# Batched matrix product in pairs: product tiles with rows of two batches, and stores of pairs in 16 KB runs

## The chip, the cores and the metric

The kernel runs on one core of a Trainium2 chip. The metric is the device time of one execution in microseconds (us); lower is better. Three runs of the kernel before the change took 125.2 to 125.29 us, with a median of 125.25 us.

Names used below: PE is the matrix engine (TensorE), DVE the vector engine, ACT the scalar engine, POOL GpSimd, and SP the engine that here only issues transfers. SBUF is the on-chip memory with 128 partitions, PSUM the memory that PE writes. DMA engines, sixteen for the core, move data between HBM and SBUF. A transfer is issued from an engine's queue: q10 in the profile is ACT's queue, q1 is SP's.

## The reference

Sixteen independent products of a 512 x 512 matrix with the transpose of another, in float32:

```python
batch, m, k, n = 16, 512, 512, 512
a = randn(batch, m, k)      # float32
b = randn(batch, n, k)      # float32
out = np.matmul(a, b.transpose(0, 2, 1)).astype(np.float32)
```

The inputs are 33.55 MB and the output 16.78 MB.

## The kernel before

The batches go in eight pairs. For a pair, `load` (line 82) brings both batches of `a` in one transfer of 2 MB and both of `b` in another. In both, SBUF partition 64e + p gets the eight consecutive rows 8p to 8p + 7 of batch e of the pair, which is one run of 16 KB; so partitions 0 to 63 belong to the first batch of the pair and 64 to 127 to the second. There are seven slots for loads (`NL`), even numbers being of `a` and odd ones of `b`. Load 1 is issued from SP, all others from ACT: seven at the start, and loads 2u + 7 and 2u + 8 by ACT in pair u, after the copies of line 157 (line 168).

DVE casts what has landed to bfloat16 (lines 130 to 134; `ha` and `wa` are the two halves of the k range of `a`, `hb` and `wb` those of `b`). PE transposes it in blocks of 128 x 128 into PSUM (`tp`, line 199), four groups of 16 transposes for a pair. ACT copies the transposed `a` to `ta` (line 157), DVE the transposed `b` to `tb` (line 144). After a transpose, the 128 columns of a block hold 64 rows of the first batch and 64 rows of the second. The copy of line 157 sorts them: it makes two copies for each block of k, one for each batch, so that in `ta` the rows of one batch stand together.

The product of a batch is made of four tiles of 128 x 512 in PSUM (`ps`, four banks), each a sum over four blocks of k, with `ta` as the stationary operand and `tb` as the moving one (line 218). A pair thus takes 32 matmuls of 128 output rows by 512 columns, the first batch of the pair (e = 0) and then the second. ACT copies each finished tile to the output buffer `ob` (line 177), sorting columns on the way. `ob` is a ring of seven batches (`NO`): before ACT writes batch n, it waits until the store of batch n - 7 has landed (line 174).

A store (line 92) is 1 MB, one for each batch, issued from SP: partition p holds four consecutive rows of the output, a run of 8 KB. SP waits for the counter `s_out`, which ACT raises twice in a pair: after the fifth tile (the first batch is then complete) and after the eighth. Before its first store SP also waits until load 7 has landed (`nc.sync.wait_ge(s_ld[0], 32)`, line 106). The store of the last batch is issued from SP after all compute (line 236).

What sets the order: each engine works through its own instructions in program order, and counters (semaphores) join them. PE's copy-back counters are `s_pv` (tiles of the first batch copied, banks of `ps` free again), `s_ea` and `s_eb` (a block of `ta` or `tb` ready), and its own are `s_mm` (a tile is complete) and `s_ta`, `s_tb` (a group is transposed). SP's queue holds nothing but load 1 and the stores, in order. ACT's holds loads, copies of `ta` and copies of `ob`.

Of the kernel before, what the change touches and what calls it, by code (L numbers as in the profile page):

```python
# [10 lines left out]
def kernel(  # L11
# [6 lines left out]
    nc = tc.nc  # L18
    P = 128
    batch, M, K = a.shape  # L20
    _, N, _ = b.shape
    J = M // P
    KO = K // P
    HP = P // 2
    HK = K // 2
    pairs = batch // 2
    f32 = mybir.dt.float32
    bf16 = mybir.dt.bfloat16
    NL = 7
    NO = 7  # L30

    def sbuf(name, shape, dtype):
        return ctx.enter_context(nc.sbuf_tensor(name, shape, dtype))

    def sem(name):
        return tc.alloc_semaphore(name)

    with tc.tile_critical(no_gpsimd_drain=True):  # L40
        ident = sbuf("ident", [P, P], bf16)
        one = sbuf("one", [P, 1], f32)
        ld = sbuf("ld", [P, NL, 2 * J, K], f32)
        ha, wa, hb, wb = (
            sbuf(name, [P, 2 * J, HK], bf16) for name in ("ha", "wa", "hb", "wb")
        )
        ta = sbuf("ta", [P, KO, 2 * J * P], bf16)
        tb = sbuf("tb", [P, KO, 2 * J * P], bf16)
        ob = sbuf("ob", [P, NO, J, N], f32)
        tp = ctx.enter_context(nc.psum_tensor("tp", [P, 4, 2 * J, P], bf16))  # L50
        ps = ctx.enter_context(nc.psum_tensor("ps", [P, 4, N], f32))

        s_set = sem("s_set")
        s_ld = [sem(f"s_ld{i}") for i in range(NL)]
        s_st = [sem(f"s_st{i}") for i in range(NO)]

        s_go = sem("s_go")
        s_wa = sem("s_wa")
# [6 lines left out]
        s_ea = sem("s_ea")  # L65
        s_eb = sem("s_eb")
        s_mm = sem("s_mm")
        s_pv = sem("s_pv")
        s_out = sem("s_out")
# [5 lines left out]
            out=ident[:], in_=ident[:], compare_op=mybir.AluOpType.not_equal, fill=1.0,  # L75
# [6 lines left out]
        def load(n, engine):  # L82
            u, slot = n // 2, n % NL
            src = (a if n % 2 == 0 else b)[2 * u:2 * u + 2].rearrange(
                "e (p j) k -> (e p) j k", j=2 * J
            )
            engine.dma_start(ld[:, slot], src).then_inc(s_ld[slot], 16)

        def landed(n):
            return s_st[n % NO], 16 * (n // NO + 1)  # L90

        def store(n):
            nc.sync.wait_ge(s_out, n + 1)
            nc.sync.dma_start(
                out[n].rearrange("(p j) n -> p j n", j=J), ob[:, n % NO]
            ).then_inc(landed(n)[0], 16)

        load(0, nc.scalar)
        load(1, nc.sync)
        for n in range(2, NL):  # L100
            load(n, nc.scalar)

        for n in range(2 * pairs):
            nc.gpsimd.wait_ge(s_ld[n % NL], 16 * (n // NL + 1)).then_inc(s_go, 1)  # L104

        nc.sync.wait_ge(s_ld[0], 32)
        for n in range(batch - 1):
            store(n)

        def taker(engine):  # L110
            return lambda s, n: engine.wait_ge(s, n).then_inc(s, -n)  # L111
# [5 lines left out]
        take = taker(nc.vector)  # L117
# [3 lines left out]
        with nc.Fori(0, pairs, engines=[dve]) as u:  # L121
            for x, (h, w, s_c, s_w) in enumerate(
                ((ha, wa, s_ca, s_wa), (hb, wb, s_cb, s_wb))
            ):
                src = ld[:, bass.ds((u * 2 + x) % NL, 1)].rearrange("p o j k -> p (o j) k")
                take(s_go, 1)
                if x == 0:
# [4 lines left out]
                    out=h[:, J:, :], in_=src[:, J:, :HK]  # L132
                ).then_inc(s_c, 1)
                nc.vector.tensor_copy(out=w[:], in_=src[:, :, HK:]).then_inc(s_w, 1)  # L134
            for ko in range(KO):
# [5 lines left out]
                if ko == 1:  # L141
# [3 lines left out]
                    out=tb[:, ko, :],  # L145
                    in_=tp[:, 2 + ko % 2].rearrange("k j p -> k (j p)"),
# [6 lines left out]
        for u in range(pairs):  # L153
            for ko in range(KO):
                nc.scalar.wait_ge(s_ta, KO * u + ko + 1)
                for e in range(2):
                    c = nc.scalar.copy(  # L157
                        out=ta[:, ko, e * J * P:(e + 1) * J * P].rearrange(
                            "k (j p h) -> k j p h", j=J, h=2
                        ),  # L160
                        in_=tp[:, ko % 2, :, e * HP:(e + 1) * HP].rearrange(
                            "k (h j) p -> k j p h", h=2
                        ),
                    )
                c.then_inc(s_ea, 1)


            for n in (2 * u + NL, 2 * u + NL + 1):
                if n < 2 * pairs:
                    load(n, nc.scalar)  # L170
            for e in range(2):
                n = 2 * u + e
                if n >= NO:
                    nc.scalar.wait_ge(*landed(n - NO))
                for j in range(J):
                    nc.scalar.wait_ge(s_mm, J * n + j + 1)
                    c = nc.scalar.copy(  # L177
                        out=ob[:, n % NO, j, :].rearrange("m (p j) -> m p j", j=2 * J),
                        in_=ps[:, j, :].rearrange("m (j p) -> m p j", j=2 * J),
                    )  # L180
                    if e == 0:
                        c.then_inc(s_pv, 1)
                    elif j in (0, J - 1):
                        c.then_inc(s_out, 1)


        pe = nc.tensor.engine
        take = taker(nc.tensor)
        with nc.Fori(0, pairs, engines=[pe]):
            with nc.Fori(0, 2, engines=[pe]):  # L190

                for x, (h, s_c, s_t, s_e) in enumerate(
                    ((ha, s_ca, s_ta, s_ea), (hb, s_cb, s_tb, s_eb))
                ):
                    take(s_c, 1)
                    for g in range(2):
                        take(s_e, 1)
                        for j in range(2 * J):
                            t = nc.tensor.transpose(  # L199
                                tp[:, 2 * x + g, j, :], h[:, j, g * P:(g + 1) * P], ident[:]  # L200
                            )
                            if x == 1 and g == 0 and j == 0:
                                t.then_inc(s_da, 1)
                        t.then_inc(s_t, 1)

            for e in range(2):
                for jj in range(0, J, 2):
                    if e == 1:  # L210
                        take(s_pv, 2)
                    for kk in range(0, KO, 2):
                        for j in (jj, jj + 1):
                            for ko in (kk, kk + 1):
                                if (e, jj, j) == (0, 0, 0) and ko >= 2:
                                    nc.tensor.wait_ge(s_ea, ko - 1)
                                    nc.tensor.wait_ge(s_eb, ko - 1)
                                t = nc.tensor.matmul(  # L218
                                    ps[:, j, :],
                                    ta[:, ko, (e * J + j) * P:(e * J + j + 1) * P],  # L220
                                    tb[:, ko, :].rearrange("k (j p) -> k j p", j=2 * J)[
                                        :, :, e * HP:(e + 1) * HP
                                    ],
                                    start=(ko == 0),
                                    stop=(ko == KO - 1),
                                )
                            if kk == KO - 2:
                                t.then_inc(s_mm, 1)

    with tc.tile_critical(sync_engine=act, no_gpsimd_drain=True):
        for n in range(batch - NO, batch - 1):
            nc.scalar.wait_ge(*landed(n))
    waits = nc.cur_bb.bb.instructions[-1]
    last = nc.sync.dma_start(
        out[batch - 1].rearrange("(p j) n -> p j n", j=J), ob[:, (batch - 1) % NO]
    )
    tc.add_manual_dep(
        last.ins,  # L240
        waits.name,
# [33 lines left out]
```

## Time and profile before

| what | value |
|---|---|
| median of three runs | 125.25 us |
| the profiled execution, its own time | 124.88 us |
| its span, first to last instruction | 123.1 us |
| PE matmuls `ps`, line 218 | 256, mean 379 ns, busy 57.8 us |
| ACT copies `ob`, line 177 | 64, mean 590 ns, busy 34.3 us |
| ACT copies `ta`, line 157 | 64, mean 613 ns, busy 33.0 us |
| PE transposes, line 199 | 512, mean about 224 ns |
| weight loads of the matmuls, line 218 | 256, mean 98 ns |
| read from HBM, written | 33.55 MB, 16.78 MB |
| ACT waiting for a store in the ring of `ob` | 3.8 us, two times |

How to read it: the span runs from the first to the last instruction; the execution's own time is 1.78 us longer. Matmuls are pipelined, so the mean of one is longer than the distance from one to the next: 32 of them end 7.29 us after the first began. Slices of the page are fortieths of the span, about 3.1 us each; a digit is a busy share in tenths. In a line of the timeline stand start, duration, engine, line, operation, output, input, count, and in brackets the idle time before and what ended it. The time of a transfer "to landing" runs from its issue to its completion.

### The profile page before, as it was taken

Reading aid. Unit: us, or ns where it says so; the run is one execution under the profiler, and the core shown is the slowest. Engines: PE = TensorE matmul, PEld = TensorE weight load, DVE = VectorE, ACT = ScalarE, POOL = GpSimd, SP = SyncE. Lnnn points to the kernel's source line nnn. Section 1 sums busy time; section 2 is a strip of 40 time slices with the busy share of each in tenths; the row PEclk is TensorE's granted clock in tenths of the full one; section 3 lists DMA queues with packets and bytes.
Section 4 is the critical chain, followed back from the end, with each engine's and each line's share of the span. In section 5 each row is a group of like instructions: output and inputs, shape, how many; then the busy total and the mean of one; then the engine's idle time right before and its main releaser. Section 6 shows DMA issues by size and latency. Waiting matters only on the chain. (4 is left out here: it accounts for less than half of the span.)

```text
span 123.1 us, 2235 instructions
## 1 busy us (share of the span) xinstructions
PE 90.1 (73%) x768; PEld 54.7 (44%) x768; DVE 67.9 (55%) x96; ACT 67.9 (55%) x130; POOL 0.7 (1%) x6
## 2 busy tenths in 40 slices
PE   0000089999999899989998999999699936997000
PEld 0000078447734764575477447644564425542000
DVE  0000598992896589388918983871987039600000
ACT  0400064567945966696589468855865184666000
POOL 2000000000000000000000000000000000000000
PEclk9999999999999999999999999999999999999965
DMA  4999999999999998999999999999999999999991
GB/s 144 394 426 431 447 437 431 426 431 426 426 431 426 426 405 373 453 399 437 407 429 426 463 405 442 437 415 434 423 418 458 399 426 423 431 429 423 426 431 45
DMA packets 4610, 50.34 MB, mean 409 GB/s; under 512 B 513, under 2 KB 513, under 8 KB 513
## 3 DMA queue, kind: packets, MB, share of 16 engines
q10 hardware_dynamic: 2160, 31.46, 60.6%
q1 hardware_dynamic: 2448, 18.88, 36.4%
q14 instruction: 2, 0.01, 0.0%
HBM read 33.55 MB, written 16.78 MB: 409 GB/s over the span
## 5 line engine op out<-in xcount | busy, mean ns | idle before, releaser
L218 PE MATMUL ps<-tb,ta 128*128 128x512 bf16 x256 | 57.8, 379 | 0.5
L177 ACT COPY ob<-ps 128x512 f32<-128x512 f32 x64 | 34.3, 590 | 26.3 <-PE ps L218 22.5
L157 ACT COPY ta<-tp 128x512 bf16<-128x512 bf16 x64 | 33.0, 613 | 15.5 <-PE tp L199 15.0
L218 PEld LDWEIGHTS ps<-tb,ta 128*128 128x128 bf16 x256 | 24.1, 98 | 30.6 <-issue 4.0
L199 PE MATMUL tp<-ident,ha 128*128 128x128 bf16 x256 | 18.5, 224 | 18.8 <-PEq L111 18.3
L199 PEld LDWEIGHTS tp<-ident,ha 128*128 128x128 bf16 x256 | 15.8, 100 | 22.3 <-issue 20.6
L144 DVE COPY tb<-tp 128x1024 bf16<-128x1024 bf16 x32 | 21.2, 685 | 3.6 <-DVEq L111 3.6
L199 PE MATMUL tp<-ident,hb 128*128 128x128 bf16 x256 | 17.5, 223 | 3.8 <-PEq L111 3.5
L199 PEld LDWEIGHTS tp<-ident,hb 128*128 128x128 bf16 x256 | 15.3, 100 | 5.0 <-issue 4.8
L130 DVE CAST ha<-ld 128x1024 bf16 x8 | 5.5, 690 | 14.6 <-POOLq L104 13.8
L139 DVE COPY ha<-wa 128x2048 bf16<-128x2048 bf16 x8 | 5.5, 691 | 12.4 <-DVEq L111 12.4
L130 DVE CAST hb<-ld 128x1024 bf16 x8 | 5.5, 689 | 8.4 <-DVEq L111 8.4
L134 DVE CAST wa<-ld 128x2048 bf16 x8 | 9.8, 1220 | 0.0
L134 DVE CAST wb<-ld 128x2048 bf16 x8 | 9.8, 1220 | 0.0
L131 DVE CAST hb<-ld 128x1024 bf16 x8 | 5.5, 687 | 0.0
L131 DVE CAST ha<-ld 128x1024 bf16 x8 | 5.5, 687 | 0.0
L143 DVE COPY hb<-wb 128x2048 bf16<-128x2048 bf16 x8 | 5.5, 684 | 0.0
L152 ACT ACT_TABLE_LOAD x1 | 1.3, 1283 | 4.1 <-issue 4.1
L74 POOL TENSOR_SCALAR_AFFINE_SELECT ident<-ident 128x128 bf16<-128x128 bf16 x1 | 0.3, 292 | 0.2 <-POOL ident L72 0.2
L72 POOL MEMSET ident<- 128x128 bf16 x1 | 0.2, 204 | 0.5 <-SPq L40 0.5
L152 ACT COPY one<-const-float32-1.0 128x1 f32<-128x1 f32 x1 | 0.2, 191 | 0.0
L259 POOL MEMSET const-bfloat16-1.0<- 128x1 bf16 x1 | 0.1, 102 | 0.0
(3 smaller groups left out, 0.3 us busy)
## 6 DMA issues: line engine op xcount, KB each, us to landing
ld<-in_a_dram ACTq DMA_DIRECT2D x8, 2048.0 KB, 29.3
out_dram<-ob SPq DMA_DIRECT2D x16, 1024.0 KB, 25.6
ld<-in_b_dram ACTq DMA_DIRECT2D x7, 2048.0 KB, 27.1
ld<-in_b_dram SPq DMA_DIRECT2D x1, 2048.0 KB, 12.6
```

Of the source, the lines that this page charges most:

```text
L74: nc.gpsimd.affine_select(out=ident[:], in_=ident[:], compare_op=mybir.AluOpType.not_equal, fill=1.0, base=0, pattern=[[-1, P]], channel_m ...
L130: nc.vector.tensor_copy(out=h[:, :J, :], in_=src[:, :J, :HK])
L131: nc.vector.tensor_copy(out=h[:, J:, :], in_=src[:, J:, :HK]).then_inc(s_c, 1)
L134: nc.vector.tensor_copy(out=w[:], in_=src[:, :, HK:]).then_inc(s_w, 1)
L139: nc.vector.tensor_copy(out=ha[:], in_=wa[:]).then_inc(s_ca, 1)
L143: nc.vector.tensor_copy(out=hb[:], in_=wb[:]).then_inc(s_cb, 1)
L144: nc.vector.tensor_copy(out=tb[:, ko, :], in_=tp[:, 2 + ko % 2].rearrange("k j p -> k (j p)"),).then_inc(s_eb, 1)
L152: nc.scalar.copy(out=one[:], in_=nc.const_aps.tensor(1.0, (P, 1), f32))
L157: c = nc.scalar.copy(out=ta[:, ko, e * J * P:(e + 1) * J * P].rearrange("k (j p h) -> k j p h", j=J, h=2), in_=tp[:, ko % 2, :, e * HP:(e ...
L177: c = nc.scalar.copy(out=ob[:, n % NO, j, :].rearrange("m (p j) -> m p j", j=2 * J), in_=ps[:, j, :].rearrange("m (j p) -> m p j", j=2 * J),)
L199: t = nc.tensor.transpose(tp[:, 2 * x + g, j, :], h[:, j, g * P:(g + 1) * P], ident[:])
L218: t = nc.tensor.matmul(ps[:, j, :], ta[:, ko, (e * J + j) * P:(e * J + j + 1) * P], tb[:, ko, :].rearrange("k (j p) -> k j p", j=2 * J)[:, ...
```

## The change

Each tile of the product now has 64 output rows of the first batch of the pair in PSUM partitions 0 to 63, and 64 rows of the second in partitions 64 to 127. Eight such tiles (`W`) make a pair. Each matmul is replaced by two of 64 output rows and 512 columns, one for each batch, with their own stationary and moving operands, which write the lower and the upper half of the same bank. The transposed `a` already has this order, so ACT copies a whole block of k of `ta` at once, 1024 columns, with no sorting. Line numbers below are those of the diff alone.

A partition of `ob` then holds, for a whole pair, eight consecutive output rows: a run of 16 KB. `ob` has the same size. It is now a ring of seven halves of pairs: half h has four of the eight rows for both batches. Stores are listed in `STORES`: a pair is stored in one transfer of 2 MB once both halves are complete; pair 3, whose halves lie at the two ends of the ring, and the last pair are stored in two halves of 1 MB (runs of 8 KB). There are ten stores instead of sixteen, with five counters (`NS`). ACT's wait for the ring names the store that holds the half written seven halves before. The wait of SP for load 7 before the first store stays.

```diff
     NL = 7
+    W = 2 * J
     NO = 7
+    NS = 5
+    STORES = []
+    for u in range(pairs):
+        if 2 * u % NO == NO - 1 or u == pairs - 1:
+            STORES += [(2 * u,), (2 * u + 1,)]
+        else:
+            STORES += [(2 * u, 2 * u + 1)]
+    OF = {h: n for n, halves in enumerate(STORES) for h in halves}
...
-        ob = sbuf("ob", [P, NO, J, N], f32)
+        ob = sbuf("ob", [P, NO * J, N], f32)
...
         def landed(n):
-            return s_st[n % NO], 16 * (n // NO + 1)
+            return s_st[n % NS], 16 * (n // NS + 1)
 
         def store(n):
-            nc.sync.wait_ge(s_out, n + 1)
-            nc.sync.dma_start(
-                out[n].rearrange("(p j) n -> p j n", j=J), ob[:, n % NO]
-            ).then_inc(landed(n)[0], 16)
+            halves = STORES[n]
+            u, lo = halves[0] // 2, halves[0] % 2 * J
+            at = halves[0] % NO * J
+            return nc.sync.dma_start(
+                out[2 * u:2 * u + 2].rearrange("e (p w) n -> (e p) w n", w=W)[
+                    :, lo:lo + len(halves) * J, :
+                ],
+                ob[:, at:at + len(halves) * J],
+            )
...
         nc.sync.wait_ge(s_ld[0], 32)
-        for n in range(batch - 1):
-            store(n)
+        for n, halves in enumerate(STORES[:-1]):
+            nc.sync.wait_ge(s_out, halves[-1] + 1)
+            store(n).then_inc(landed(n)[0], 16)
...
                 nc.scalar.wait_ge(s_ta, KO * u + ko + 1)
-                for e in range(2):
-                    c = nc.scalar.copy(
-                        out=ta[:, ko, e * J * P:(e + 1) * J * P].rearrange(
-                            "k (j p h) -> k j p h", j=J, h=2
-                        ),
-                        in_=tp[:, ko % 2, :, e * HP:(e + 1) * HP].rearrange(
-                            "k (h j) p -> k j p h", h=2
-                        ),
-                    )
+                c = nc.scalar.copy(
+                    out=ta[:, ko, :], in_=tp[:, ko % 2].rearrange("k j p -> k (j p)")
+                )
                 c.then_inc(s_ea, 1)
...
-            for e in range(2):
-                n = 2 * u + e
-                if n >= NO:
-                    nc.scalar.wait_ge(*landed(n - NO))
-                for j in range(J):
-                    nc.scalar.wait_ge(s_mm, J * n + j + 1)
+            for j in range(W):
+                h = 2 * u + j // J
+                if j % J == 0 and h >= NO:
+                    nc.scalar.wait_ge(*landed(OF[h - NO]))
+                nc.scalar.wait_ge(s_mm, W * u + j + 1)
...
+            for jj in range(0, W, 2):
+                if jj >= J:
+                    take(s_pv, 2)
+                for kk in range(0, KO, 2):
+                    for j in (jj, jj + 1):
+                        for ko in (kk, kk + 1):
...
+                            for e in range(2):
+                                half = slice(e * HP, (e + 1) * HP)
                                 t = nc.tensor.matmul(
-                                    ps[:, j, :],
-                                    ta[:, ko, (e * J + j) * P:(e * J + j + 1) * P],
-                                    tb[:, ko, :].rearrange("k (j p) -> k j p", j=2 * J)[
-                                        :, :, e * HP:(e + 1) * HP
-                                    ],
+                                    ps[half, j % 4, :],
+                                    ta[:, ko, j * P + e * HP:j * P + (e + 1) * HP],
+                                    tb[:, ko, :].rearrange("k (j p) -> k j p", j=W)[:, :, half],
                                     start=(ko == 0),
                                     stop=(ko == KO - 1),
                                 )
...
-        for n in range(batch - NO, batch - 1):
+        for n in range(len(STORES) - 1 - NS, len(STORES) - 1):
             nc.scalar.wait_ge(*landed(n))
...
-    last = nc.sync.dma_start(
-        out[batch - 1].rearrange("(p j) n -> p j n", j=J), ob[:, (batch - 1) % NO]
-    )
+    last = store(len(STORES) - 1)
```

More of the change, by code (lines that the diff above doesn't have):

```diff
@@ L54 @@
         s_ld = [sem(f"s_ld{i}") for i in range(NL)]
-        s_st = [sem(f"s_st{i}") for i in range(NO)]
+        s_st = [sem(f"s_st{i}") for i in range(NS)]
         s_go = sem("s_go")
@@ L170 @@
                     load(n, nc.scalar)
-            for e in range(2):
-                n = 2 * u + e
-                if n >= NO:
-                    nc.scalar.wait_ge(*landed(n - NO))
-                for j in range(J):
-                    nc.scalar.wait_ge(s_mm, J * n + j + 1)
-                    c = nc.scalar.copy(
-                        out=ob[:, n % NO, j, :].rearrange("m (p j) -> m p j", j=2 * J),
-                        in_=ps[:, j, :].rearrange("m (j p) -> m p j", j=2 * J),
-                    )
[L181 to L184, printed above, removed]
+            for j in range(W):
[3 more added lines that the diff above has]
+                nc.scalar.wait_ge(s_mm, W * u + j + 1)
+                c = nc.scalar.copy(
+                    out=ob[:, h % NO * J + j % J, :].rearrange("m (p j) -> m p j", j=W),
+                    in_=ps[:, j % 4, :].rearrange("m (j p) -> m p j", j=W),
+                )
+                if j < J:
+                    c.then_inc(s_pv, 1)
+                elif j in (J, W - 1):
+                    c.then_inc(s_out, 1)
         pe = nc.tensor.engine
@@ L204 @@
                         t.then_inc(s_t, 1)
[L208 to L218, printed above, removed]
-                                    ps[:, j, :],
-                                    ta[:, ko, (e * J + j) * P:(e * J + j + 1) * P],
-                                    tb[:, ko, :].rearrange("k (j p) -> k j p", j=2 * J)[
-                                        :, :, e * HP:(e + 1) * HP
-                                    ],
+            for jj in range(0, W, 2):
[4 more added lines that the diff above has]
+                        for ko in (kk, kk + 1):
+                            if j == 0 and ko >= 2:
+                                nc.tensor.wait_ge(s_ea, ko - 1)
+                                nc.tensor.wait_ge(s_eb, ko - 1)
+                            for e in range(2):
+                                half = slice(e * HP, (e + 1) * HP)
+                                t = nc.tensor.matmul(
+                                    ps[half, j % 4, :],
+                                    ta[:, ko, j * P + e * HP:j * P + (e + 1) * HP],
+                                    tb[:, ko, :].rearrange("k (j p) -> k j p", j=W)[:, :, half],
                                     start=(ko == 0),
@@ L226 @@
                                 )
-                            if kk == KO - 2:
-                                t.then_inc(s_mm, 1)
+                        if kk == KO - 2:
+                            t.then_inc(s_mm, 1)
     with tc.tile_critical(sync_engine=act, no_gpsimd_drain=True):
-        for n in range(batch - NO, batch - 1):
+        for n in range(len(STORES) - 1 - NS, len(STORES) - 1):
             nc.scalar.wait_ge(*landed(n))
     waits = nc.cur_bb.bb.instructions[-1]
-    last = nc.sync.dma_start(
-        out[batch - 1].rearrange("(p j) n -> p j n", j=J), ob[:, (batch - 1) % NO]
-    )
+    last = store(len(STORES) - 1)
     tc.add_manual_dep(
```

## The prediction

> **What bounds the kernel now.** I read the engine shares and the slices of the page first, then the DMA queues, first over the whole span and then in two windows, and last the timeline around the final pair.
>
> ```profile
> span 123.1 us, 2235 instructions
> ...
> PE 90.1 (73%) x768; PEld 54.7 (44%) x768; DVE 67.9 (55%) x96; ACT 67.9 (55%) x130; POOL 0.7 (1%) x6
> ...
> DMA  4999999999999998999999999999999999999991
> GB/s 144 394 426 431 447 437 431 426 431 426 426 431 426 426 405 373 453 399 437 407 429 426 463 405 442 437 415 434 423 418 458 399 426 423 431 429 423 426 431 45
> ...
> out_dram<-ob SPq DMA_DIRECT2D x16, 1024.0 KB, 25.6
> ```
>
> No compute engine is full, while the 16 DMA engines are busy in every slice but the first and the last. 50.34 MB at about 430 GB/s are 117 us, so the transfers are the bound. A store waits 25.6 us from issue to landing, ten times what it needs alone (1.049 MB / 426 GB/s = 2.46 us): there is a long backlog. The question for any change is whether it keeps that backlog until the end.
>
> The two queues share the engines as the next two windows show: first 3 to 12 us, where loads of 16 KB rows stand in both queues, then 50 to 95 us, where q10 has loads (16 KB rows) and q1 stores (8 KB rows). Columns: packets, MB, share.
>
> ```profile
> q1 hardware_dynamic: 118, 1.93, 50.5%
> q10 hardware_dynamic: 113, 1.84, 48.3%
> ```
>
> ```profile
> q10 hardware_dynamic: 880, 12.85, 67.1%
> q1 hardware_dynamic: 879, 6.41, 33.8%
> ```
>
> Turns are taken packet by packet (880 against 879), and a packet is one row. Equal rows mean equal shares; 16 KB beside 8 KB mean two to one for the loads. The loads win that race now, and what follows the last of them is this (timeline):
>
> ```profile
> 98.80 2.05 ACT L177 COPY ob<-ps 128x512 f32<-128x512 f32 x4 [3.07 <-DMA out_dram<-ob]
> 100.41 0.69 DVE L130 CAST hb<-ld 128x1024 bf16 x1 [4.77 <-DVEq L111]
> 105.83 7.29 PE L218 MATMUL ps<-tb,ta 128*128 128x512 bf16 x32
> 111.06 1.07 ACT L177 COPY ob<-ps 128x512 f32<-128x512 f32 x2 [0.71 <-PE ps L218]
> 113.98 0.33 SPq L236 DMA_DIRECT2D out_dram<-ob  x1
> ```
>
> The last load ends at 99.7 us (last packet in the trace; landing 100.07). From there 13.9 us of compute pass until the last store is issued. The DMA engines are full all that time with stores queued before: 99.7 to 121.6 us at 426 GB/s are 9.4 MB, nine stores. The 3.07 us wait on a store shows that the ring of output buffers is full, that is, the backlog is as large as it can be.
>
> [...] 16 transposes took 1.87 us at the start and 1.05 us from 19.5 us on, and the granted clock fell about 5 us after the last matmul.
>
> **The change part by part.**
>
> *Store rows of 16 KB, bytes alone.* Six stores of 2 MB have 16 KB rows; four of 1 MB keep 8 KB (pairs 3 and 7). Loads alone move 430 GB/s (15 to 40 us), 8 KB stores alone 426 (101 to 118 us). 12.58 MB x (1/426 - 1/430) = 0.27 us gained. It counts only while the engines have work.
>
> *The same rows, share.* A 2 MB store beside loads now takes half: 4.19 MB / 428 GB/s = 9.8 us for it and for the load beside it, where a load took 7.35 us beside a 1 MB store. Schedule, from the first store packet (46.8 us, held by the wait at line 106 for load 7, which stays): stores of pairs 0, 1, 2 end at 56.6, 66.4, 76.2; the two halves of pair 3, at the old shares, at 83.6 and 90.9; pair 4 at 100.7; pair 5 at 110.5. All are ready in time: PE's period is 11.47 us (33.04 to 44.51), so pair 4 is ready about 75, and pair 5, whose matmuls wait for load 11, about 91. Loads: 8 ends at 48.8, then 9 to 15 at 58.6, 68.3, 77.6, 84.9, 92.7, 102.5 and 112.3, each 9.8 us beside a 16 KB store and 7.35 beside an 8 KB one. The last load thus ends 12.6 us later than 99.7, having given way to stores that were not urgent.
>
> *The tail.* Pair 6 needs load 13 (92.7) and is ready at 92.7 + 0.37 landing + 0.34 to the cast + 5.42 to the matmuls (100.41 to 105.83) + 8.0 to its last copy = 106.8; its store follows at 110.5, shares 1.8 us with load 15, and is done at 116.3. Then nothing is left to transfer. Pair 7: 112.3 + 0.37 + 0.34 + 5.42 puts its matmuls at 118.4; its first half is stored 5.84 us later (111.67 against 105.83), 124.3; first packet 1.0 us later (as for load 0, 0.94 to 1.93), so DMA idles about 9 us, 116.3 to 125.3. Two halves of 2.46 us end at 130.2; receipt and end take 1.5 us (121.6 to 123.1). Span 131.7.
>
> *Copies of `ta`.* One of 1024 columns for two of 512. From 613 ns for 512 columns and 191 ns for one column (L152), 1024 should take about 191 + 2 x 422 = 1035 ns, and two pipelined ones take 1.07 us: a gain of 0 to 0.1 us each, inside PE's transposes. I take zero. In the tail it stands beside hb's DVE chain.
>
> *Matmuls.* 512 of 64 output rows for 256. Each still streams 512 columns, now 32 pitches of about 222 ns a pair (7.12 us). Side by side, the time is unchanged; one after another it is 14.2 us. Issue is no limit: a transpose and its weight load have a pitch of about 55 ns, so two take 110 of the 222 ns. [...] I take 0.3 us, paid once, in the tail; for the other pairs a matmul block up to 9.5 us is covered, since 21.6 + 7 x (9.5 + 4.35) = 118.5 is when load 15 releases the last pair.
>
> *PE's clock.* PE idles from the transposes of pair 7's `ha` (about 106) to those of `hb` (about 114), longer than the 5 us after which the clock fell. Cold transposes hide beside DVE's chain (pair 0, cold, also needs 5.42 us from hb's cast at 16.15 to its matmuls at 21.57). If the clock is back before the matmuls it costs nothing[...]. I take 0.7.
>
> *Later release, coarser waits.* SP waits for both halves, holding the first half of a pair back 2.3 us; before 100 us the backlog hides it. ACT's ring waits name the store of a pair: half 13 needs the store ended at 83.6, half 14 the one at 90.9; all are past. SP queues nothing but stores behind its waits. Zero. The 3.8 us of ring waits vanish; they were hidden.
>
> Sum: 131.7 + 0.3 + 0.7 = 132.7 span. The profiled execution was 124.88 for a span of 123.1, so 134.5; the median shown, 125.25, is 0.37 above it: 134.9 us.
>
> **Rivals.**
> 1. *As above, loads starved, tail bare*: 134.9, own range 131.5 to 139 (unknowns: tiling 0 to 9.5 us blocks[...]). For it: the packet counts.
> 2. *PE becomes the bound.* Weight loads exposed by 50 ns each (half of the 98 ns of the row) give blocks of 10.3 us: matmuls of pair 7 at 21.6 + 7 x 14.65 = 124.1, end about 142.6. Fully serial halves: period 18.6, pair 7 at 151.8, about 174. For it: no tiled matmul in the trace[...]. Against: [...] weight loads that already hide here.
> 3. *Not slower.* The shares stay two to one, because the 16 KB run goes out in smaller packets or is weighed by bytes. It decides at one point: between the end of load 15 and the first packet of half 14 lie 0.37 + 0.34 + 5.42 + 5.84 + 1.0 = 13.0 us, or 5.5 MB, so with the last two stores 7.6 MB must still be queued; load 15 must end by 121.6 - 17.9 = 103.7. It then ends about 99.7, the bare gain of 0.27 remains: 125.0, or 125.3 if packets are cut. Against: loads of the same 2 MB shape show 16 KB packets in q1.
>
> **How the numbers follow.** Chances: first 0.76, second 0.18 (0.06 up to 144, 0.12 beyond), third 0.06. The likeliest gives 134.9. The range 129.5 to 144 holds nearly all of the first and a third of the second. About 0.2% (0.25 us) is what this kernel's measurement can tell from none: faster 0.04 and same 0.02 from the third, slower 0.94.
>
> **What would show it.** Right: in windows after 47 us both queues near 50% with equal MB; last cast of `hb` near 113; a hole in the DMA row from about 116 to 125; ACT no longer waiting for stores. Starvation wrong: hb's last cast near 100 and a DMA row full to the end. Tiling wrong: the matmul block of a pair above 9.5 us, PE busy throughout with no gaps. I would be wrong on size if the last pair takes other than 13.7 us from its last load to its last issue, or a backlog survives 112 us.

## The result, and the profile after

The changed kernel takes 135.01 us, the median of four runs (134.64 to 135.65), against 125.27 us before: a ratio of 1.078, with a 95% interval of 1.074 to 1.083. The profiled execution took 135.03 us for a span of 133.2 us, 10.1 us more than before.

The page of the changed kernel, with the span, the slices of PE, of its granted clock and of DMA, and the groups of the product:

```profile
span 133.2 us, 2708 instructions
...
PE   0000489998999999899999806999279950299920
...
PEclk9999999999999999999999975799999998559995
DMA  4999999999999999999999999999999999700095
GB/s 152 413 438 428 438 428 438 423 433 423 443 413 428 315 384 443 413 438 421 443 423 438 413 443 423 435 418 445 418 438 423 443 418 443 305 10 0 0 398 231
...
L231 PE MATMUL ps<-tb,ta 128*64 128x512 bf16 x512 | 57.8, 380 | 0.0
...
L174 ACT COPY ta<-tp 128x1024 bf16<-128x1024 bf16 x32 | 30.8, 1015 | 31.7 <-PE tp L210 31.7
L231 PEld LDWEIGHTS ps<-tb,ta 128*64 128x64 bf16 x512 | 33.3, 110 | 21.5 <-issue 3.1
```

Where the DMA row was full to the end, it now has a hole near the end: slices of 10, 0 and 0 GB/s. Up to there the rate is about the old one, but for a dip from 43 to 50 us (315 and 384 GB/s). In the trace no packet moves between 117.60 and 126.76 us, 9.2 us; the profiled executions differ by 10.15 us. PE has new gaps as well ("06", "27", "502"): its transposes wait for casts of late loads (DVE sits idle for 19.7 us before the casts of `hb`, 8.4 us in the kernel before).

The queues of the changed kernel from 50 to 75 us (packets, MB, share) show the cause:

```profile
q1 hardware_dynamic: 361, 5.39, 50.5%
q10 hardware_dynamic: 359, 5.36, 50.2%
```

Packets still alternate one for one (361 and 359), but a store's packet is now as large as a load's (both 16 KB, 611 ns each at the median; one of 8 KB took 309 ns), so loads have half the engines (50.2%) where they had two thirds (67.1%). The last load ends at 113.2 us instead of 99.7 (counted, as in the prediction, to the last of the sixteen 4-byte packets that follow each transfer in the trace and are called its marks below; its last row of data ends at 112.6 us). What follows it, in the timeline of the changed kernel:

```profile
107.43 1.07 PE L210 MATMUL tp<-ident,ha 128*128 128x128 bf16 x16
114.03 0.69 DVE L148 CAST hb<-ld 128x1024 bf16 x1 [6.78 <-DVEq L129]
115.63 1.86 PE L210 MATMUL tp<-ident,hb 128*128 128x128 bf16 x16 [7.13 <-PEq L129]
117.36 1.87 PE L210 MATMUL tp<-ident,ha 128*128 128x128 bf16 x16
119.03 1.20 PE L210 MATMUL tp<-ident,hb 128*128 128x128 bf16 x16
120.16 7.22 PE L231 MATMUL ps<-tb,ta 128*64 128x512 bf16 x64
126.99 1.07 ACT L188 COPY ob<-ps 128x512 f32<-128x512 f32 x2 [0.60 <-PE ps L231]
```

Much the same compute stands behind the last load as before: 14.0 us from the cast of `hb` to the last copy (114.03 to 128.06), against 13.4 (100.41 to 113.80). Before, nine stores were still to be moved in the tail (the stretch after the last load) and filled it; now the stores of all pairs but the last end at 117.6 us. The windows of the changed kernel (start and end, length, then busy time and instructions of PE, PEld, DVE, ACT, POOL, then clock, DMA share, GB/s) put the hole beside a busy PE:

```profile
112.00:117.60 5.60, 1.97 (x19) 1.89 (x20) 3.57 (x5) 0.00 (x0) 0.00 (x0) 0.54 0.67 287
117.60:126.00 8.40, 8.40 (x86) 6.02 (x85) 2.64 (x5) 4.76 (x8) 0.00 (x0) 0.90 0.00 0
126.00:132.00 6.00, 1.38 (x14) 0.60 (x10) 0.00 (x0) 1.47 (x3) 0.00 (x0) 0.80 0.85 350
```

So in the hole the bound is the chain of casts, transposes and matmuls of the last pair, and before it the bound is DMA: the two used to overlap and now stand one after the other.

### The profile page after: what moved, and what is told of

It is laid out like the page before. It is cut to its first block, busy times and chain, and to the rows that moved or that the text cites. A ratio compares the mean times of both kernels' runs of the same rounds, so it can differ in the third digit from the quotient of the medians.

```text
span 133.2 us, 2708 instructions
## 1 busy us (share of the span) xinstructions
PE 95.0 (71%) x1024; PEld 67.7 (51%) x1024; DVE 68.4 (51%) x96; ACT 66.0 (50%) x98; POOL 0.7 (1%) x6
## 5 line engine op out<-in xcount | busy, mean ns | idle before, releaser
L231 PE MATMUL ps<-tb,ta 128*64 128x512 bf16 x512 | 57.8, 380 | 0.0
L174 ACT COPY ta<-tp 128x1024 bf16<-128x1024 bf16 x32 | 30.8, 1015 | 31.7 <-PE tp L210 31.7
L231 PEld LDWEIGHTS ps<-tb,ta 128*64 128x64 bf16 x512 | 33.3, 110 | 21.5 <-issue 3.1
L210 PE MATMUL tp<-ident,ha 128*128 128x128 bf16 x256 | 20.0, 240 | 17.0 <-PEq L129 17.0
L210 PE MATMUL tp<-ident,hb 128*128 128x128 bf16 x256 | 19.8, 239 | 15.4 <-PEq L129 14.8
L210 PEld LDWEIGHTS tp<-ident,ha 128*128 128x128 bf16 x256 | 17.2, 108 | 20.9 <-issue 20.6
L210 PEld LDWEIGHTS tp<-ident,hb 128*128 128x128 bf16 x256 | 17.5, 108 | 16.8 <-issue 16.8
L148 DVE CAST hb<-ld 128x1024 bf16 x8 | 5.5, 690 | 19.7 <-DVEq L129 19.7
L157 DVE COPY ha<-wa 128x2048 bf16<-128x2048 bf16 x8 | 5.5, 690 | 10.1 <-DVEq L129 10.1
## 6 DMA issues: line engine op xcount, KB each, us to landing
out_dram<-ob SPq DMA_DIRECT2D x6, 2048.0 KB, 21.9
```

What stands on the lines that cost most here:

```text
L148: nc.vector.tensor_copy(out=h[:, :J, :], in_=src[:, :J, :HK])
L157: nc.vector.tensor_copy(out=ha[:], in_=wa[:]).then_inc(s_ca, 1)
L174: c = nc.scalar.copy(out=ta[:, ko, :], in_=tp[:, ko % 2].rearrange("k j p -> k (j p)"))
L210: t = nc.tensor.transpose(tp[:, 2 * x + g, j, :], h[:, j, g * P:(g + 1) * P], ident[:])
L231: t = nc.tensor.matmul(ps[half, j % 4, :], ta[:, ko, j * P + e * HP:j * P + (e + 1) * HP], tb[:, ko, :].rearrange("k (j p) -> k j p", j=W) ...
```

## The experiments

Three theories were put to the test. Shares: the 16 KB rows of the stores take bandwidth from the loads, the last load is late, and the tail is bare (nothing is left to transfer). Tiles: the column-tiled product (two matmuls of 64 output rows in the halves of a bank) costs the time. Release: the stores of whole pairs come too late or are too large.

### The new product with rows of 8 KB

```diff
-        if 2 * u % NO == NO - 1 or u == pairs - 1:
+        if True:
             STORES += [(2 * u,), (2 * u + 1,)]
...
-    NS = 5
+    NS = 7
```

> The changed kernel with its column-tiled product, but every half of a pair stored on its own (1 MB, runs of 8 KB), as soon as it is complete. Shares theory (16 KB store rows take half of the DMA engines from the loads, so the last load ends late and the tail has nothing left to transfer): the two-to-one split is back, the last load ends near 100 us instead of 112.6, no hole in the DMA row, and the time is that of the kernel before, 125.3 us (125.0 to 125.8). Tiles theory (the column-tiled product is what costs): 134 to 135 us, since the product is unchanged. Release theory (the first half of a pair is held back until the second is complete, and transfers are twice as large): 125.3 us.

Measured: 125.45 us, median of 20 runs, against 125.08 us for the kernel before in the same comparison: 1.0029 (1.0017 to 1.0040). Its queues from 50 to 95 us, and the DMA row of its page:

```profile
q10 hardware_dynamic: 878, 12.81, 66.8%
q1 hardware_dynamic: 881, 6.43, 33.9%
```

```profile
DMA  4999999999999999999999999999999999999990
```

The old shares are back, the row is full, the last load ends at 99.6 us instead of 113.2, and nearly all of the loss is gone although the product is that of the changed kernel. The tiles theory falls: about 0.3% (0.4% at the end of the interval) belongs to all the rest of the change together. (`NS`, the number of counters for stores, grows with the number of stores.) The release theory forecast the same time, so this run doesn't tell it from the shares theory.

### The same, released by pairs

```diff
-            nc.sync.wait_ge(s_out, halves[-1] + 1)
+            nc.sync.wait_ge(s_out, halves[-1] // 2 * 2 + 2 if halves[-1] < batch - 2 else batch - 1)
```

> As e1_rows8_by_half (rows of 8 KB, two transfers of 1 MB for a pair), but both transfers of a pair wait until the whole pair is complete, as in the changed kernel. Shares theory: 125.3 us (125.0 to 125.8), the release costs nothing. Release theory: 134 to 135 us. Tiles theory: 134 to 135 us.

Measured: 125.46 us, 20 runs, 1.0033 (1.0021 to 1.0045) of the kernel before. Holding the first half of a pair back costs nothing that can be told from the run above (125.45 us). The half of the release theory that speaks of lateness falls; transfers of 1 MB say nothing of the half that speaks of size, on which the two-pair run and the held stores below bear.

### The kernel before, with loads in rows of 8 KB

This is the mirror image: product and stores of the kernel before stay, and the loads' rows are made as small as the stores'. The counts of the waits on loads double (line 104, line 106).

```diff
-            engine.dma_start(ld[:, slot], src).then_inc(s_ld[slot], 16)
+            for lo in (0, J):
+                engine.dma_start(
+                    ld[:, slot, lo:lo + J], src[:, lo:lo + J]
+                ).then_inc(s_ld[slot], 16)
```

> The kernel before with its product and its stores untouched; only each load of 2 MB is issued as two transfers of 1 MB with rows of 8 KB. Shares theory: rows of both queues are now equal (8 KB), stores get half of the engines, the last load ends near 111 us and the same tail follows with a hole of some 9 us: 134 us (132 to 136). Tiles theory and release theory: neither is touched, so 125.3 us plus 33.55 MB x (1/426 - 1/430) = 0.7 us for smaller rows: 126 us.

Measured: 133.68 us, 1.069 (1.066 to 1.072) of the kernel before. Its queues from 50 to 95 us, and its slices:

```profile
q1 hardware_dynamic: 1319, 9.63, 50.7%
q10 hardware_dynamic: 1316, 9.60, 50.6%
```

```profile
DMA  4999999999999999999999999999999997960095
GB/s 112 416 426 429 429 421 421 421 424 424 419 424 421 421 424 426 421 431 429 424 426 434 421 424 431 429 424 424 436 419 431 424 431 324 376 262 0 0 424 214
```

The kernel before gets most of the loss of the changed one (8.6 us; 9.7 there), hole included (117.38 to 125.0 us without a packet in the trace), from its loads alone: the last one ends at 112.1 us instead of 99.7. What decides is the ratio of the two queues, not 16 KB as such.

In all these runs the size of a transfer changes together with its rows (2 MB with 16 KB, 1 MB with 8 KB), so the times alone don't tell rows from transfers. The traces do: in each of the fifteen stretches of 1 us from 60 to 75 us, in the kernel before as in the changed one, packets of both queues start, while a whole transfer of 1 MB takes 2.45 us with nothing beside it (the first marks of successive stores after 100 us in the kernel before). Turns are thus not taken by whole transfers.

### One pair, then two pairs, in rows of 8 KB

```diff
-        if 2 * u % NO == NO - 1 or u == pairs - 1:
+        if 2 * u % NO == NO - 1 or u in (0, pairs - 1):
...
-    NS = 5
+    NS = 7
```

> The changed kernel, but pair 0 is also stored as two halves of 1 MB with rows of 8 KB; pairs 1, 2, 4, 5 and 6 keep rows of 16 KB. Shares theory, by the schedule of the prediction (7.35 us for a load beside 8 KB stores, 9.8 us beside 16 KB): stores end at 61.5 (pair 0), 71.3, 81.1, 95.8 (pair 3), 105.6; loads 9 to 15 at 55.6, 63.5, 73.3, 82.6, 90.0, 97.9, 107.7. The last load ends 4.6 us earlier than the 112.3 of that schedule, the hole shrinks by as much, and 135.0 becomes 130.4 us (129.5 to 131.5). Were the cost tied to the number of large transfers or to their release, one of six fewer would give 135.0 - 9.6 / 6 = 133.4 us.

Measured: 130.14 us, 1.037 (1.033 to 1.041) of the kernel before. With `u in (0, 1, pairs - 1)`:

> As e3a_one_pair_split, with pairs 0 and 1 stored as halves with rows of 8 KB; pairs 2, 4, 5 and 6 keep rows of 16 KB. Shares theory, same schedule: the last load ends at 102.7 us, which is before the 103.7 us that the prediction names as the point up to which the tail stays covered; so almost no hole and 125.0 to 126.3 us, though four of the six large transfers are still there. Were the cost in proportion to the large transfers: 135.0 - 2 x 9.6 / 6 = 131.8 us.

Measured: 125.68 us, 17 runs, 1.0041 (1.0028 to 1.0053). The DMA rows of the two pages, one pair split and two:

```profile
DMA  4999999999999999999999999999999999970094
```

```profile
DMA  4999999999999999999999999999999999999394
```

The hole shrinks from 9.2 to 5.3 us (117.13 to 122.40) and then to part of one slice, and the last load ends at 108.2 and 103.5 us, where the schedule of the prediction gives 107.7 and 102.7. The time falls 4.9 us with the first pair split and 4.5 with the second; in proportion to the number of large transfers it would have fallen 1.6 each time. A pair that is stored in 16 KB rows before the last load has ended lets one load of 2 MB past, in 8 KB rows two; so each pair changed should bring the last load forward by one load, 2.10 MB at 430 GB/s or 4.9 us (an estimate), until the tail is covered. It came forward by 5.0 and 4.7 us.

### The changed kernel with its stores held back

```diff
-        nc.sync.wait_ge(s_ld[0], 32)
         for n, halves in enumerate(STORES[:-1]):
+            m = (7, 9, 11, 13, 13, 15)[min(n, 5)]
+            nc.sync.wait_ge(s_ld[m % NL], 16 * (m // NL + 1))
             nc.sync.wait_ge(s_out, halves[-1] + 1)
```

> The changed kernel with its 16 KB rows, and SP's waits before stores altered: the stores of pairs 0, 1, 2 also wait until loads 7, 9, 11 have landed, the two halves of pair 3 for load 13, all later ones for load 15. Shares theory: two loads move for each pair stored, the last load ends at 100 to 103 us, at least 7.6 MB of stores are still queued then, and no hole follows: 125.0 to 125.6 us, with at best the 0.27 us of larger rows below the kernel before. Tiles theory: 134 to 135 us. Release theory: stores start later still, so 135 us or more.

Measured: 125.89 us, 1.0058 (1.0037 to 1.0080), 0.3 us above the range named. Rows, transfers and product are those of the changed kernel; only the waits give the loads their share back, and 9 of the 9.7 us are recovered. The release theory, which asked for 135 us or more, falls here in both halves, since the transfers of whole pairs are as large as in the changed kernel and start later. The last load ends at 100.6 us, and the DMA row has no hole:

```profile
DMA  4999999999999998999999999999999979999993
```

About a microsecond seemed to be left in a dip (the digit 7, a slice from 98.9 to 102.0 us), where load 15 ends and the next store still waits for it. So that wait was moved to load 14:

```diff
-            m = (7, 9, 11, 13, 13, 15)[min(n, 5)]
+            m = (7, 9, 11, 13, 13, 14)[min(n, 5)]
```

> As e5_stores_held, but the stores from pair 4 on wait for load 14 instead of load 15, so that they are in the queue when the last load ends. In e5_stores_held the DMA row had one hole of about 1 us there (the slice with digit 7, from 100.3 us). Shares theory: that hole closes and the rest stays, 125.89 - 1.0 = 124.9 us (124.6 to 125.3), at or slightly below the 125.08 us of the kernel before in that comparison. If the hole came from something other than the wait for load 15: 125.9 us again.

Measured: 125.85 us, 1.0056 (1.0036 to 1.0076): a miss. The dip did close. The window from 100 to 102 us, first with the wait for load 15, then for load 14:

```profile
100.00:102.00 2.00, 2.00 (x27) 1.30 (x22) 0.59 (x1) 2.00 (x5) 0.00 (x0) 1.00 0.63 262
```

```profile
100.00:102.00 2.00, 2.00 (x22) 1.03 (x20) 0.63 (x2) 1.07 (x2) 0.00 (x0) 1.00 1.05 442
```

Yet the time stayed. The sixteen engines don't end together. With the wait for load 14, their marks of completion for the last store run from 120.22 to 122.49 us; with the wait for load 15, from 121.65 to 122.16. In the dip, engines that were ahead stood idle, while the slowest was still moving the second half of pair 3 (the marks of that store run from 100.57 to 102.44 us with the dip, and it lands at 102.9 us in both). This fits a dip that was no loss on the engine that sets the end; it rests on one trace of each run. Neither version beats the kernel before, and no run here shows the 0.27 us that the larger rows were reckoned to bring. Why both stay 0.4 us above the new product with rows of 8 KB (125.45 us) was not tried.

## Why the prediction was right

The forecast was 134.9 us, and the mechanism was the likeliest of its cases; the experiments confirm it from four sides (rows back, loads smaller, part of the rows, waits).

- *Shares.* Each 2 MB store took 9.7 us beside a load (landings of pairs 0, 1, 2 at 58.7, 68.4, 78.1 us; 9.8 predicted). Right.
- *End of the last load.* 112.3 predicted, 113.2 measured on the slowest engine. The DMA engines moved less around the first store than before: 287 GB/s from 44 to 48 us, against 369. That is 0.76 us at 430 GB/s. The two runs with held stores, whose first store is the same, have 373 and 344 there, so the row size alone doesn't explain it; the cause is open.
- *The tail.* 5.42 us from `hb`'s cast to the matmuls plus 0.7 for PE's clock were predicted, 6.13 measured. The part for the clock was a guess that rested on no trace, so that it fits this well is luck. Its way was not the one described: the prediction thought cold transposes (at the lower clock) hidden and the matmuls at risk, but the matmul block ran in 7.22 us, and it was the last transposes, 1.87 and 1.20 us a group instead of 1.05, that came late. It had read pair 0 as a cold case that also needs 5.42 us; but there the clock rose at 19.1 us, while the first transposes of `hb` ran (17.73 to 19.42 us), and the two groups behind them took 1.05 us each. In the tail the clock rose only at 119.3 us. The hole was to last from 116.3 to 125.3 and lasted from 117.6 to 126.8.
- *Matmuls.* 64 half matmuls take 7.22 us, where 32 whole ones took 7.29: the two halves run side by side. Weight loads of 64 columns take 110 ns, no less than the 98 ns of 128 columns, and hide: the block that holds 64 of them takes the 7.22 us. PE's period in the first pairs is 11.60 us (21.59 to 33.19) against 11.47. The trace before held no matmul of 64 rows, so the 0.3 us taken for tiling and the second rival's block times were the author's estimates: at most 0.13 of the 0.3 us is there, and the second rival is out.
- *Copies of `ta`.* 1015 ns each (1035 reckoned), outside the bound, as said.
- *Bytes alone.* The 0.27 us did not appear in any run with both large rows and a covered tail (125.68, 125.89, 125.85 us). They all have the new product too, which costs 0.37 us with small rows, so this doesn't show that the gain is absent.
- *The point of decision.* Load 15 had to end by 103.7 us. At 103.5 us (two pairs split) the cost is 0.4%, at 108.2 it is 3.7%. Beyond the point the loss follows the lateness: last loads 4.5, 8.4 and 9.5 us past it (one pair split, small loads, the changed kernel) go with losses of 5.0, 8.6 and 9.7 us. The point holds.

Apart from the 0.9 us of the last load, the terms were off by 0.3 us at most, and partly cancel: span 132.7 predicted, 133.2 measured. A further 0.37 us was added because the median before lay that much above its profiled execution; here the median lies 0.02 us below it (135.01 and 135.03). So that 134.9 comes within 0.1 us is in part luck; the mechanism and the size of each main term are not. A slip without effect: 21.9 us at 426 GB/s are 9.3 MB, not 9.4.

Left open: the new product, stored in runs of 8 KB, costs 0.3% (125.45 against 125.08 us) with shares and tail as before. The runs of a half lie 16 KB apart in the output where a batch's lay together, and the marks of the last store spread over 1.9 us (120.10 to 122.02) instead of 1.4 (120.22 to 121.60). Which of the two, if either, is the cause was not tried.

## What to carry to other kernels

Where two queues stood before the same DMA engines in these runs, row size was priority: each got the engines in proportion to its row (67% to 34% for 16 KB beside 8 KB, 50% each for equal rows of 16 or of 8 KB). Before enlarging the rows of a queue, ask which of the two is urgent. Loads that feed a long last computation must end early, and the stores that can wait are what covers that computation; reckon how many bytes have to be queued when the last load ends, and look at that number rather than at the mean rate, which here stayed near 430 GB/s until the hole, but for the dip at the first store.

## What the runs showed of the hardware that was not expected

- The engines don't end together. The marks of the last load run over 1.4 us before (98.27 to 99.70) and over 2.5 us in the changed kernel (110.66 to 113.20); in both, fourteen of the sixteen lie within 0.8 us and two come late. With the dip the marks of the last store lay 0.5 us apart, without it 2.3. Closing such a dip need not gain anything (125.89 and 125.85 us).
- PE's clock fell sooner than the 5 us that the prediction took from the trace before (118.08 us, 4.96 us after the last matmul). In the changed kernel it was halved from 78.4 to 85.2 us, 2.1 us after the last transpose (76.24), and again from 112.5 to 119.3, 4.0 us after the last of PE's work ahead of it (108.50), each 6.83 us. In the new product with rows of 8 KB it fell for 3.4 us, in a tail in which PE idled only 1.9 us before the transposes of `hb`:

```profile
99.00:103.20 4.20, 2.09 (x34) 1.77 (x32) 2.85 (x4) 3.00 (x6) 0.00 (x0) 1.00 1.00 419
103.20:106.60 3.40, 2.92 (x28) 2.95 (x29) 2.04 (x5) 2.76 (x3) 0.00 (x0) 0.50 1.01 426
```

  The length of a gap alone doesn't decide: in the kernel before, PE idled 2.61 us in the tail (99.39 to 102.00 us), and the clock stayed at 1.00 until 118.08. In its trace the clock stood at full for 98.99 us; in that of the changed kernel the stretches between changes of the clock last 58.03, 6.83, 27.31, 6.83 and 10.24 us. These six are 29, 17, 2, 8, 2 and 3 times 3.41 us (10.24 less 6.83). Cut into pieces of that length from the first rise of the clock, the two traces have four halvings; in the piece ahead of each, the records of matmuls and transposes fill between 0 and 1.28 us. In every other whole piece at full clock they fill 1.75 us or more. So a piece need not be idle to be followed by a halving. This is what two traces show; what makes the clock fall is not shown.
